# A two-layer RWKV-7 / mLSTM trunk on one core: group norm of a block at once, sums taken a step later, another order of addresses

## The chip, the core and the metric

The program runs on one core of a Trainium2 chip. A core has a matrix engine (PE, its weight loads are PEld), three engines for elementwise work (DVE, ACT, POOL), a queue that starts most transfers (SP), and 16 DMA engines. Each engine takes its instructions in the order in which they were written for it and waits on semaphores for the others. The metric is the device time of one execution in microseconds (us). Three runs of the kernel before took 2931.28, 2917.58 and 2933.17 us; the median is 2931.28 us.

## The reference

All of it is float32. The sequence is 1024 long, the width is 1024, there is one batch and there are two layers. A layer is a mixer and a SwiGLU feed-forward (FFN), each behind a modulated norm; layer 0 mixes by RWKV-7, layer 1 by a chunkwise mLSTM.

```
c_act = silu(c)
for i in 0, 1:
    sh1, sc1, g1, sh2, sc2, g2 = split(c_act @ ada_w[i] + ada_b[i], 6)   # modulation, a row of 6 x 1024
    x = x + g1 * mixer_i(rms(x) * (1 + sc1) + sh1)
    h = rms(x) * (1 + sc2) + sh2
    x = x + g2 * ((silu(h @ Wg) * (h @ Wu)) @ Wd)                       # inner width 2816
return rms(x) * final_w

# the end of the RWKV-7 mixer: a group norm over each head of 64
mu = mean(y, -1);  var = mean((y - mu)^2, -1)
y = (y - mu) * rsqrt(var + 64e-5) * gn_w + gn_b
out = ((y + bonus) * gate) @ w_out
```

## The kernel before, in words

Activations lie feature by position in tiles of 128 x 512: eight feature tiles `kt` and two halves of the sequence (`hf`, lists `x[0]` and `x[1]`). A float32 product is made of three passes over rounded parts: `split` (L209) writes a rounded copy on ACT (L211) and the remainder on DVE (L212), and `product` (L894) multiplies high by high, low by high and high by low. Weights come through the tile `wraw`, and their two parts lie in `wq` (or `whi`, `wlo`).

The stages follow each other in this order, by time in the profiled run:

- 0 to 305 us: modulation of layer 0, norms, projections of RWKV.
- 305 to 1019 us: the loop `chunks` (L1450). It has 19 steps. In step i the stages `rw_prep`, `rw_inverse`, `rw_solve`, `rw_chain` and `rw_finish` (L800) work on blocks i, i-1, i-2, i-3 and i-3, each 128 x 512; 16 blocks in all. Between the stages a generator of filler products (`fillers`, L1421) is run up to a quota: projections, and at the end the first FFN blocks that are computed ahead by `first` (L962) for half 0 alone, how many by the table `EARLY`.
- 1019 to 1680 us: output projection and FFN of layer 0 (`ffn`, L1064). Gate and up products are made by a scheme with seven sub-products (`seven`, L904) over tiles X[1] to X[7], which are sums and differences of quarter tiles, with weights from `wpair` (L865). Then comes `down` (L1003), again with seven sub-products.
- 1680 to 2141 us: mLSTM. 2141 to 2917 us: projection, FFN of layer 1 and the last norm (`final`, L1413).

Work that is not urgent runs as a background generator `self.bg`, a step at a time between weight loads: `sums` (L982) prepares weights for `down`, and `ada(s)` (L293) computes one sixth of the modulation of layer 1. `ada` loads 128 x 256 pieces of `ada_w`, adds them up on DVE with `c` as the factor (L305, L307; eight pieces to a sum), and sums over partitions with a small matmul against ones into the tile `tr`. It uses the tile `bgs` in the FFN stages and `st` in the others (`spare`, L289). `rstd` (L322) makes a norm: squares on ACT (L329) added on DVE (L330), four matmuls into `sc`, a power on POOL (L336), four more matmuls into `sc`.

`rw_finish` takes the 128 x 512 block `Ys`, eight groups of 64 columns. The mean comes from a reduction on DVE (L806). Then ACT makes the squares group by group with a summed output (L809, eight instructions and eight reads of the accumulator), POOL the power (L811), and ACT scales and shifts group by group (L814, eight instructions).

What sets the order: the program is written through a layer that gives each instruction a priority by its place in the program (parts under `ahead` are moved forward by the table `AHEAD`) and then lists each engine's instructions; a tile that is needed again waits for the last reader of whatever had its address. The tables `ROOM` and `FROOM` name the tiles of a phase with copies and columns; addresses are dealt out in the order of the table, so that a table's order says which tile of the next phase lies over which tile of the last. `phase` changes between them.

Of the kernel before, what the change touches and what calls it, by code (L numbers as in the profile page):

```python
# [9 lines left out]
F32 = mybir.dt.float32  # L10
# [7 lines left out]
P = 128  # L18
D = 1024
T = 1024  # L20
KT = 8
# [3 lines left out]
EARLY = ((0, 5, 8), (0, 0, 3))  # L25
# [20 lines left out]

RES = {"x": (8, 520)}
ROOM = {"wraw": (2, 1024), "whi": (2, 1024), "wlo": (2, 1024), "a": (18, 512), "KB": (1, 1024), "AT": (1, 512), "Z": (1, 512),
# [5 lines left out]
        "msq": (4, 2)}  # L54

FROOM = {"wraw": (3, 1024), "wq": (5, 2048), "w4": (2, 1024), "gb": (11, 1024), "bgs": (1, 1024), "tt": (5, 512),
# [73 lines left out]
class K:  # L130
# [158 lines left out]
    def spare(self):  # L289

        return self.t("bgs" if "bgs" in self.pools else "st", [P, 4, 256])

    def ada(self, s):  # L293

        nc = self.nc
        w, n = 256, 2
        for f in range(0, D, w):
            room = self.spare()
            t = room[:, 0]
            for kt in range(KT):  # L300
                m = room[:, 1 + kt % 3]
                nc.sync.dma_start(m, self.A["ada1"][kt, :, s * D + f:s * D + f + w])
                ca = self.ca[:, kt:kt + 1]
                if kt == 0:
                    nc.vector.tensor_scalar(t, m, ca, None, MUL)  # L305
                else:
                    nc.vector.scalar_tensor_tensor(t, m, ca, t, MUL, ADD)  # L307
                if kt % 2 and kt < KT - 1:
                    yield
            pt = self.bank("tr", [P, n])  # L310
            for q in range(n):
                self.mm(pt[:, q:q + 1], t[:, q * P:q * P + P], self.k_("ones"))
            u = 8 * s + f // P
            o = CI["adab1"] + u
            nc.vector.scalar_tensor_tensor(self.mod[1][:, u:u + n], pt, float(D), self.cc[:, o:o + n], MUL, ADD)
            if s in (1, 4):
                o = (0 if s == 1 else 8) + f // P
                nc.vector.tensor_scalar(self.scp[1][:, o:o + n], self.mod[1][:, u:u + n], 1.0, None, ADD)
            yield


    def rstd(self, xs):  # L322
# [477 lines left out]
    def rw_finish(self, S):  # L800
# [4 lines left out]
        m, v, jk = (self.t(n, [P, 64 if n == "gj" else 8]) for n in ("gm", "gv", "gj"))  # L805
# [879 lines left out]
```

## Time and profile before

| | |
|---|---|
| median of three runs | 2931.28 us (2917.58 to 2933.17) |
| the profiled execution | 2919.56 us |
| its span in the trace | 2917.8 us |
| PE / PEld busy | 2702.9 us (93%) / 2124.4 us |
| DVE / ACT / POOL busy | 2036.1 / 1401.1 / 74.5 us |
| moved by DMA | 492.38 MB, mean 169 GB/s |

The span is the time from the first instruction to the last; the profiled execution is 1.8 us longer than its span. Busy is the time in which an engine has an instruction at work, so 2917.8 less 2702.9, that is 214.9 us, is PE's idle time. [...] A row of the timeline that ends in brackets names how long the engine had been idle before it and what it waited for.

### The profile page before, as it was taken

How to read it: one execution, taken by the hardware profiler on the slowest of the kernel's cores; microseconds unless marked ns; L12 is line 12 of the kernel's file. 1: busy time of each engine (PE TensorE's matmuls, PEld its weight loads, DVE VectorE, ACT ScalarE, POOL GpSimd, SP SyncE). 2: the span in 40 equal slices, each digit the busy share in tenths (PEclk: the TensorE clock that was granted, in tenths of full speed). 3: DMA queues.
4: the chain of work that ended last, by engine and by line, in shares of the span. 5: the costliest groups of instructions: out<-in, count | busy, mean ns of one | idle time of the engine just before them, and what ended most of it. 6: DMA issues, size and time to landing. Idle time of an engine off the chain costs nothing.

```text
span 2917.8 us, 46574 instructions
## 1 busy us (share of the span) xinstructions
PE 2702.9 (93%) x17080; PEld 2124.4 (73%) x17080; DVE 2036.1 (70%) x4029; ACT 1401.1 (48%) x2641; POOL 74.5 (3%) x98
## 2 busy tenths in 40 slices
PE   6899889999898999999999989999989999999988
PEld 5576556677676677887777767778867788887776
DVE  7877776877676468788877677665556865667645
ACT  5766786777666554322244354233435433323433
POOL 0000000000000000000000000000000000000000
PEclk9899789999798999999999989889989999999999
DMA  8775444455543455577788744345264322347734
GB/s 293 262 266 149 121 128 125 119 158 145 155 138 102 134 199 163 187 228 233 243 276 258 229 138 129 121 152 159 94 205 146 106 100 94 107 138 246 237 118 150
DMA packets 359721, 492.38 MB, mean 169 GB/s; under 512 B 125212, under 2 KB 208796, under 8 KB 359492
## 3 DMA queue, kind: packets, MB, share of 16 engines
q1 hardware_dynamic: 345668, 464.24, 50.1%
q10 hardware_dynamic: 13824, 25.17, 2.4%
q8 instruction: 134, 2.20, 0.3%
q14 instruction: 95, 0.78, 0.1%
HBM read 359.77 MB, written 129.50 MB: 168 GB/s over the span
## 4 chain that ended last, share of the span: by engine, by line
PE 61%; DVE 14%; DMA 11%; ACT 6%; issue 6%; POOL 1%; SPq 1%; DVEq 0%; POOLq 0%; ACTq 0%
PE dn L207 23%; PE c L207 20%; PE iv L207 7%; PE px L207 7%; PE sc L207 2%; DMA wraw<-wsd 2%; DMA tt<-gd 1%; DMA wraw<-in_wdn 1%; DVE wq L212 1%; DMA bgs<-in_ada 1%; DVE ga L212 1%; ACT wq L211 1%; DVE wlo L212 1%; PE tr L207 1%; ACT whi L211 1%
## 5 line engine op out<-in xcount | busy, mean ns | idle before, releaser
L207 PE MATMUL dn<-a,whi 128*128 128x512 f32 (+1 forms) x1200 | 434.4, 428 | 20.4 <-ACT a L211 8.0
L211 ACT ACTIVATE wq<-wraw 128x1024 fp32r<-128x1024 f32 x202 | 210.7, 1057 | 335.4 <-DVE wraw L889 89.6
L207 PE MATMUL c<-ga,wq 128*128 128x512 f32 x1446 | 354.2, 394 | 8.6 <-ACT ga L211 7.8
L207 PEld LDWEIGHTS c<-ga,wq 128*128 128x128 f32 x1446 | 271.5, 189 | 73.7 <-ACT ga L211 10.1
L212 DVE TENSOR_TENSOR wq<-wraw,wq 128x1024 fp32r<-128x1024 f32 x202 | 244.3, 1221 | 85.3 <-ACT wq L211 85.1
L207 PEld LDWEIGHTS dn<-a,whi 128*128 128x128 f32 (+1 forms) x1200 | 226.3, 196 | 81.8 <-ACT a L211 10.7
L207 PE MATMUL dn<-a,wlo 128*128 128x512 f32 (+1 forms) x664 | 275.1, 425 | 5.8 <-ACT wlo L443 2.9
L207 PE MATMUL c<-gb,wq 128*128 128x512 f32 x894 | 220.9, 399 | 9.4 <-DVE wq L212 6.4
L207 PEld LDWEIGHTS c<-gb,wq 128*128 128x128 f32 x894 | 169.2, 191 | 49.5 <-DVE wq L212 7.6
L207 PEld LDWEIGHTS dn<-a,wlo 128*128 128x128 f32 (+1 forms) x664 | 128.8, 197 | 37.1 <-issue 4.8
L211 ACT ACTIVATE whi<-wraw 128x1024 fp32r<-128x1024 f32 (+2 forms) x96 | 100.4, 1046 | 113.2 <-PE dn L207 81.9
L212 DVE TENSOR_TENSOR wlo<-wraw,whi 128x1024 fp32r<-128x1024 f32 (+2 forms) x96 | 116.0, 1208 | 45.7 <-ACT whi L211 39.7
L207 PE MATMUL iv<-ga,wq 128*128 128x512 f32 x552 | 136.0, 389 | 0.0
L207 PE MATMUL px<-ga,wq 128*128 128x512 f32 x528 | 128.7, 389 | 0.0
L211 ACT ACTIVATE w<-wraw 128x384 fp32r<-128x384 f32 (+1 forms) x100 | 56.7, 567 | 139.9 <-PE c L207 62.3
L207 PEld LDWEIGHTS iv<-ga,wq 128*128 128x128 f32 x552 | 103.6, 188 | 21.6
L207 PEld LDWEIGHTS px<-ga,wq 128*128 128x128 f32 x528 | 99.1, 188 | 20.7
L207 PE MATMUL dn<-gb,wq 128*128 128x512 f32 x426 | 104.1, 396 | 5.0 <-ACT gb L211 4.7
L207 PE MATMUL iv<-gb,wq 128*128 128x512 f32 x432 | 104.7, 390 | 0.0
L207 PEld LDWEIGHTS dn<-gb,wq 128*128 128x128 f32 x426 | 81.1, 191 | 23.9 <-ACT gb L211 5.3
L207 PE MATMUL c<-ga,w 128*128 128x512 f32 x372 | 93.4, 393 | 1.1 <-DVE ga L212 0.7
L1124 ACT ACTIVATE x<-x 128x512 f32<-128x512 f32 x77 | 48.3, 629 | 95.0 <-DVE x L933 44.9
(607 smaller groups left out, 5643.5 us busy)
## 6 DMA issues: line engine op xcount, KB each, us to landing
wraw<-in_wgu SPq DMA_DIRECT2D x110, 512.0 KB, 3.5
tt<-gd SPq DMA_DIRECT2D x154, 256.0 KB, 4.1
KT<-in_ada SPq DMA_DIRECT2D x40, 512.0 KB, 5.3
gd<-x SPq DMA_DIRECT2D x77, 256.0 KB, 2.0
gd<-tt SPq DMA_DIRECT2D x72, 256.0 KB, 2.1
wraw<-wsd SPq DMA_DIRECT2D x32, 512.0 KB, 4.7
bgs<-in_ada SPq DMA_DIRECT2D x96, 128.0 KB, 3.3
wraw<-in_wdn SPq DMA_DIRECT2D x24, 512.0 KB, 4.4
```

The costliest lines, as they stand in the source:

```text
L207: return self.nc.tensor.matmul(out, lhsT, rhs, start=start, stop=stop, **kw)
L211: self.nc.scalar.activation(hi, src, AF.Copy)
L212: self.nc.vector.tensor_tensor(lo, src, hi.bitcast(F32), SUB)
L1124: nc.scalar.activation(t, t, AF.Silu)
```

## The change

Five things are changed. (1) `rw_finish` subtracts the mean from the whole block with one DVE instruction, squares it with one ACT instruction into a `pt` tile, reduces with one DVE instruction, and scales with one DVE instruction. (2) `ada` works in pieces of 128 x 128, two to a transfer, and takes each sum over partitions one step later, beside the next column's pieces. (3) `rstd` becomes a generator `rstd_steps`, whose three parts are put between products: in `ffn` between the products of the projection and of `first`, which became a generator too; in `down`, for `final`, between the last sub-products. The weights of the first `seven` are made (`wpair`) before X[4]. (4) The tables `ROOM` and `FROOM` are in another order, and in the mLSTM stage `x[1]` lies in `SA` and `pt` and no longer in `SR`. (5) `EARLY` computes six blocks ahead in the chunk loop (five before) and three in the FFN. The argument `halves` of `ml_so` changes nothing that is issued, since its test is never true.

```diff
-EARLY = ((0, 5, 8), (0, 0, 3))
+EARLY = ((0, 6, 9), (0, 0, 3))
-ROOM = {"wraw": (2, 1024), "whi": (2, 1024), "wlo": (2, 1024), "a": (18, 512), "KB": (1, 1024), ...
+ROOM = {"a": (18, 512), "mt": (3, 512), "AR": (4, 1024), "KT": (4, 1024), "wraw": (2, 1024), "whi": (2, 1024),
+        "wlo": (2, 1024), "st": (1, 1024), "ld": (3, 512), "KB": (1, 1024), ...
-FROOM = {"wraw": (3, 1024), "wq": (5, 2048), "w4": (2, 1024), "gb": (11, 1024), "bgs": (1, 1024), "tt": (5, 512),
+FROOM = {"gb": (11, 1024), "wraw": (3, 1024), "tt": (5, 512), "wq": (5, 2048), "w4": (2, 1024), "bgs": (1, 1024),
          "ga": (17, 1024), "rs": (1, 4)}
     def ada(self, s):
-        w, n = 256, 2
-        for f in range(0, D, w):
-            room = self.spare()
...
+        room = self.spare([P, 8, P])
+        def total(f):
+            pt = self.bank("tr", [P, 1])
+            self.mm(pt, room[:, f % 2], self.k_("ones"))
...
+        for f in range(KT):
+            t = room[:, f % 2]
+            for kt in range(0, KT, 2):
+                o = 2 + 2 * (kt // 2 % 3)
+                nc.sync.dma_start(room[:, o:o + 2], self.A["ada1"][kt:kt + 2, :, s * D + f * P:s * D + f * P + P]
+                                  .rearrange("k p w -> p k w"))
+                for k in range(2):
+                    m, ca = room[:, o + k], self.ca[:, kt + k:kt + k + 1]
+                    if kt + k == 0:
+                        nc.vector.tensor_scalar(t, m, ca, None, MUL)
+                    else:
+                        nc.vector.scalar_tensor_tensor(t, m, ca, t, MUL, ADD)
+                if kt % 4 == 2:
                     yield
...
+            if f:
+                total(f - 1)
+        yield
+        total(KT - 1)
-    def rstd(self, xs):
+    def rstd_steps(self, xs):
...
             nc.vector.tensor_tensor(acc, acc, sq, ADD)
+        yield
         pc = self.bank("sc", [P, 4])
...
         nc.gpsimd.tensor_tensor(r, r, self.mhalf[:, 0:4], POW)
+        yield
...
+        yield ps
+    def rstd(self, xs):
+        *_, ps = self.rstd_steps(xs)
         return ps
@@ rw_finish
         nc.vector.tensor_reduce(m, y3, mybir.AxisListType.X, ADD)
         nc.vector.tensor_scalar(m, m, -1.0 / 64, None, MUL)
-        for q in range(8):
-            nc.scalar.activation(jk, y3[:, q, :], AF.Square, bias=m[:, q:q + 1], accum_out=v[:, q:q + 1])
+        nc.vector.tensor_tensor(y3, y3, m[:, :, None].to_broadcast([P, 8, 64]), ADD)
+        sq = self.t("pt", [P, 8, 64])
+        nc.scalar.activation(sq, y3, AF.Square)
+        nc.vector.tensor_reduce(v, sq, mybir.AxisListType.X, ADD)
         nc.vector.tensor_scalar(v, v, 1.0 / 64, GN_EPS, MUL, ADD)
         nc.gpsimd.tensor_tensor(v, v, self.mhalf, POW)
-        nc.vector.tensor_tensor(m, m, v, MUL)
-        for q in range(8):
-            nc.scalar.activation(y3[:, q, :], y3[:, q, :], AF.Identity, bias=m[:, q:q + 1], scale=v[:, q:q + 1])
+        nc.vector.tensor_tensor(y3, y3, v[:, :, None].to_broadcast([P, 8, 64]), MUL)
@@ down
                     self.add_to(l, x, n, ps[n], to[p])
+                    next(rest, None)
...
             if p == 4:
-                done(0)
-        done(1)
+                rest = done(0)
+                next(rest, None)
+        for _ in done(1):
+            pass
@@ ffn
         if l == 1:
             self.store(0, x[0])
-            r = self.rstd(x[0])
-        second()
-        if l == 1:
-            self.norm_blocks(x[0], l, r)
+            r = self.rstd_steps(x[0])
+            for _ in range(2):
+                next(r)
+                next(two)
+            self.norm_blocks(x[0], l, next(r))
...
-        with self.ahead("norm"):
-            r = self.rstd(x[1])
+        r = self.rstd_steps(x[1])
...
+        head = some()
+        for _ in range(2):
+            next(r)
+            next(head)
+        run(head)
+        r = next(r)
...
+        order = [*range(n1, NH), *range(n1)]
+        w = wgu[l]
+        head = self.wpair(w[order[0]], w[order[0] + NH], order[0] >= n1)
         X[4] = []
...
-            sil = self.seven(self.wpair(w[n], w[n + NH], not there), X, "x", p[0])
+            sil = self.seven(head or self.wpair(w[n], w[n + NH], not there), X, "x", p[0])
+            head = None
@@ rooms
+        if ml:
+            return [t for _ in range(3) for t in self.two("SA", F32)] + [self.t("pt") for _ in range(2)]
```

What the change does to the order shows at three places. The first is PE in the FFN of layer 0, where the products of `first` end and `seven` begins; before, `dn_12314` is the last product of `first`, and `c_2025`, `iv_12437` and `c_2032` are of `seven`:

```order
L207 MATMUL dn_12314<-gb_11993,wq_12310 128x512 x3
L207 MATMUL dn_12314<-gb_11996,wq_12310 128x512 x3
L207 MATMUL dn_12314<-gb_11999,wq_12310 128x512 x3
L207 MATMUL c_2025_12422<-gb_11978,wq_12406 128x512 x2
L207 MATMUL iv_12437<-gb_11990,wq_12406 128x512 x2
L207 MATMUL c_2032_12494<-ga_12348,w_2022_12409 128x512 x2
```

Now, where `c_2016`, `c_2017` and the `dn` that follow are still of `first`, and `iv_12293` with the weights `wq_12220` is of `seven`:

```order
L208 MATMUL c_2016_12146<-gb_11553,wq_12143 128x512 x3
L208 MATMUL c_2016_12146<-gb_11556,wq_12143 128x512 x3
L208 MATMUL iv_12293<-gb_11559,wq_12220 128x512 x2
L208 MATMUL c_2017_12147<-gb_11559,wq_12143 128x512 x3
L208 MATMUL c_2017_12147<-gb_11562,wq_12143 128x512 x3
L208 MATMUL c_2017_12147<-gb_11565,wq_12143 128x512 x3
```

The first two matmuls of `seven` have moved ahead of the last 36 matmuls of `first`.

The second is the SP queue at the end of the mLSTM stage, where the results `yd` of both halves are stored (`yd_81`, `yd_82`) and the projection's inputs are loaded from `yd_81` into `tt`; before:

```order
L1372 DMA yd_81<-tmp_21025 128x512
L218 DMA wraw_21312<-in_wmo 128x1024
L218 DMA wraw_21343<-in_wmo 128x1024
L218 DMA wraw_21374<-in_wmo 128x1024
L218 DMA wraw_21405<-in_wmo 128x1024
L218 DMA wraw_21436<-in_wmo 128x1024
L218 DMA wraw_21467<-in_wmo 128x1024
L1372 DMA yd_82<-tmp_21119 128x512
L1372 DMA yd_82<-tmp_21127 128x512
L833 DMA tt_21210<-yd_81 128x512
```

Now:

```order
L1406 DMA yd_81<-tmp_21066 128x512
L847 DMA tt_21251<-yd_81 128x512
L847 DMA tt_21256<-yd_81 128x512
L847 DMA tt_21261<-yd_81 128x512
L847 DMA tt_21266<-yd_81 128x512
L847 DMA tt_21271<-yd_81 128x512
L219 DMA wraw_21353<-in_wmo 128x1024
L219 DMA wraw_21384<-in_wmo 128x1024
L219 DMA wraw_21415<-in_wmo 128x1024
L1406 DMA yd_82<-tmp_21160 128x512
```

Five loads of `tt` moved ahead of the last two stores of `yd_82`.

The third is ACT between the chunk loop and the projection, whose first matmuls read `ga_11692` (now `ga_11585`), while `gb` is for `first`; before:

```order
L211 ACTIVATE wq_11732<-wraw_11730 128x1024
L211 ACTIVATE gb_11978<-x_9249 128x512
L211 ACTIVATE gb_11981<-x_9251 128x512
L211 ACTIVATE gb_11984<-x_9253 128x512
L211 ACTIVATE gb_11987<-x_9255 128x512
L211 ACTIVATE ga_11692<-tt_11690 128x512
```

Now, from the seventh of eight `gb` on (`wq_11625` and six `gb` stand ahead of them):

```order
L212 ACTIVATE gb_11565<-x_9131 128x512
L212 ACTIVATE gb_11568<-x_9133 128x512
L212 ACTIVATE wq_11656<-wraw_11654 128x1024
L212 ACTIVATE wq_11687<-wraw_11685 128x1024
L212 ACTIVATE wq_11718<-wraw_11716 128x1024
L212 ACTIVATE ga_11585<-tt_11583 128x512
```

Four `gb` and three `wq` have moved ahead of the first `ga`.

## Rows read from the trace of the kernel before

**Rows 1.** The page, parts 1 and 4: engines, chain that ended last
```profile
PE 2702.9 (93%) x17080; PEld 2124.4 (73%) x17080; DVE 2036.1 (70%) x4029; ACT 1401.1 (48%) x2641; POOL 74.5 (3%) x98
...
PE 61%; DVE 14%; DMA 11%; ACT 6%; issue 6%; POOL 1%; SPq 1%; DVEq 0%; POOLq 0%; ACTq 0%
```

**Rows 2.** Stretches: us, busy PE, PEld, DVE, ACT, POOL, PEclk, DMA, GB/s
```profile
305.00:1019.00 714.00, 650.76 (x7350) 473.82 (x7349) 508.74 (x1307) 490.68 (x1197) 33.40 (x29) 0.91 0.45 131
1140.00:1413.00 273.00, 272.08 (x1189) 221.47 (x1188) 225.28 (x364) 76.02 (x100) 0.00 (x0) 1.00 0.67 217
1413.00:1660.00 247.00, 234.42 (x1002) 188.49 (x1001) 181.50 (x311) 96.02 (x140) 0.00 (x0) 0.97 0.80 261
1740.00:1865.00 125.00, 113.07 (x594) 91.35 (x595) 96.41 (x222) 45.14 (x79) 4.20 (x8) 0.91 0.41 127
1735.80:1749.50 13.70, 7.04 (x18) 5.25 (x19) 11.12 (x25) 6.02 (x9) 0.00 (x0) 0.50 0.42 119
2285.30:2288.70 3.40, 3.40 (x10) 2.65 (x9) 2.90 (x5) 0.56 (x2) 0.00 (x0) 0.51 0.00 0
```

**Rows 3.** Waits of PE, 305 to 1020: us, times, longest
```profile
PE c L207 <- ACT Ys L797: 7.5, 7, 4.5
PE iv L207 <- ACT Y L726: 6.4, 8, 1.1
PE c L207 <- DVE VU L787: 5.1, 7, 1.3
...
PE tr L817 <- ACT Ys L814: 4.0, 5, 1.5
```

**Rows 4.** Groups of 305 to 1020 (last two: whole span): busy, mean ns
```profile
L814 ACT ACTIVATE Ys<-Ys,gm,gv 128x64 f32<-128x64 f32 x128 | 45.5, 428 | 18.4 <-DVE gm L812 18.2
L809 ACT ACTIVATE gj<-Ys,gm 128x64 f32<-128x64 f32 x128 | 43.9, 343 | 11.2 <-DVE gm L807 9.0
L809 ACT ACTIVATION_READ_ACCUMULATOR gj<-Ys,gm 128x1 f32 x128 | 24.1, 188 | 0.0
L330 DVE TENSOR_TENSOR mt<-mt,mt 128x512 f32<-128x512 f32 x35 | 24.1, 688 | 2.1 <-ACT mt L329 0.9
L329 ACT ACTIVATE tt<-ga 128x512 f32<-128x512 f32 x21 | 13.0, 620 | 19.2 <-DVE ga L1058 16.6 <-DVE ga L841 2.5
```

**Rows 5.** Timeline of PE: start, us, instruction [idle before <-releaser]
```profile
1025.82 0.79 PE L207 MATMUL c<-ga,wq 128*128 128x512 f32 x1 [7.05 <-ACT ga L211]
1114.17 4.14 PE L207 MATMUL c<-gb,wq 128*128 128x512 f32 x10 [3.39 <-DVE wq L212]
1134.78 2.73 PE L207 MATMUL c<-gb,wq 128*128 128x512 f32 x6 [2.11 <-DVE x L933]
2284.28 3.34 PE L207 MATMUL c<-gb,wq 128*128 128x512 f32 x9 [3.04 <-DVE wq L212]
```

**Rows 6.** Line L307 (first row), line L1305 (second): xcount, duration ns min/median/max
```profile
L307 DVE SCALAR_TENSOR_TENSOR bgs<-bgs,ca x84: 472/480/487, 1418.7 to 1660.4; 128x256 f32<-128x256 f32 x84
L1305 DVE SCALAR_TENSOR_TENSOR pt<-sc,gj,br x32: 340/342/351, 1808.4 to 2111.6; 128x128 f32<-128x128 f32 x32
```

**Rows 7.** Waits of PE over the whole span, the sums of the modulation
```profile
PE tr L207 <- DVE bgs L307: 6.3, 4, 2.8
...
PE tr L207 <- DVE st L307: 3.1, 4, 1.4
```

**Rows 8.** Timeline of PE at the start and the end of the mLSTM stage
```profile
1740.22 1.22 PE L207 MATMUL dn<-AR,VU 128*128 128x512 f32 x2 [6.81 <-ACT VU L211]
2145.56 4.67 PE L207 MATMUL dn<-gb,wq 128*128 128x512 f32 x12 [4.73 <-ACT gb L211]
```

**Rows 9.** Timeline of three engines around the last norm of the first half
```profile
2833.30 2.32 SPq L1032 DMA_DIRECT2D tt<-gd  x5
...
2835.10 1.84 PE L207 MATMUL sc<-kc,bgs 128*128 128x1 f32 x8 [8.47 <-DVE bgs L330]
2836.30 0.63 ACT L211 ACTIVATE gb<-tt 128x512 fp32r<-128x512 f32 x1 [2.07 <-DMA tt<-gd]
```

More of the change, by code (lines that the diff above doesn't have):

```diff
@@ L287, in ada_rows, with spare @@
                 yield
-    def spare(self):
-        return self.t("bgs" if "bgs" in self.pools else "st", [P, 4, 256])
+    def spare(self, shape):
+        return self.t("bgs" if "bgs" in self.pools else "st", shape)
     def ada(self, s):
         nc = self.nc
-        w, n = 256, 2
-        for f in range(0, D, w):
-            room = self.spare()
[L299 to L308, printed above, removed]
-                    yield
[L310 to L319, printed above, removed]
@@ L976, in first @@
             out.append(t)
+            yield
         g, u = out
@@ L1026, in down @@
         ps = [None] * 4
+        rest = iter(())
         for i, p in enumerate((1, 6, 7, 2, 4, 5, 3)):
@@ L1068, in ffn @@
         _, n0, n1 = EARLY[l]
+        two = second()
         if l == 1:
             self.store(0, x[0])
-            r = self.rstd(x[0])
-        second()
-        if l == 1:
-            self.norm_blocks(x[0], l, r)
+            r = self.rstd_steps(x[0])
[3 more added lines that the diff above has]
+            self.norm_blocks(x[0], l, next(r))
         b11, b21 = self.parts(x[0][:4], "gb"), self.parts(x[0][4:], "gb")
+        for _ in two:
+            pass
         self.store(1, x[1])
-        with self.ahead("norm"):
-            r = self.rstd(x[1])
+        r = self.rstd_steps(x[1])
         tags = "tt", "tt"
@@ L1083, in some, with run @@
             if n0 < n1:
-                self.first(l, n0, b11 + b21, tags)
                 n0 += 1
-        some()
+                yield from self.first(l, n0 - 1, b11 + b21, tags)
+        def run(it):
+            for _ in it:
+                pass
+        head = some()
[4 more added lines that the diff above has]
+        r = next(r)
         X = {1: b11, 2: b21}
@@ L1096, in ffn @@
             X[6] += self.parts(f[3][kt:kt + 1], "ga")
-        some()
+        run(some())
         X[5] = self.parts(f[1], "ga")
@@ L1102, in ffn @@
             X[7] += self.parts(f[0][kt:kt + 1], "ga")
-        some()
+        run(some())
+        order = [*range(n1, NH), *range(n1)]
+        w = wgu[l]
+        head = self.wpair(w[order[0]], w[order[0] + NH], order[0] >= n1)
         X[4] = []
@@ L1108, in ffn @@
         while n0 < n1:
-            some()
+            run(some())
         self.rate = rates[0]
         self.background(2)
-        for n in chain(range(n1, NH), range(n1)):
+        for n in order:
             there = n < n1
-            w = wgu[l]
             p = [None] * 2
@@ L1271, in ml_v, with ml_so @@
         return va
-    def ml_so(self, n, hs):
+    def ml_so(self, n, hs, halves=(0, 1), out=None):
         wt = self.weights(self.A["wo"][n])
-        out = self.two("SR", F32)
-        for hf in range(2):
+        out = out or self.two("SR", F32)
+        for hf in halves:
             ps = self.bank("dn")
@@ L1414, in final @@
         nc = self.nc
-        r = self.rstd(xs[4:] + xs[:4] if hf else xs)
+        for r in self.rstd_steps(xs[4:] + xs[:4] if hf else xs):
+            if r is None:
+                yield
         for kt in range(KT):
@@ L1446, in fillers @@
         for n in range(EARLY[0][0], EARLY[0][1]):
-            self.first(0, n, hp, ("mt", "tmp"))
-            yield 11
+            for _ in self.first(0, n, hp, ("mt", "tmp")):
+                yield 5.5
     def chunks(self, x0):
@@ L1501, in load, with rooms @@
         return x
-    def rooms(self, hf):
+    def rooms(self, hf, ml=False):
         if hf == 0:
             return [self.t("x") for _ in range(KT)]
-        return [t for _ in range(4) for t in self.two("ga" if "ga" in self.pools else "SR", F32)]
+        if "ga" in self.pools:
+            return [t for _ in range(4) for t in self.two("ga", F32)]
+        if ml:
+            return [t for _ in range(3) for t in self.two("SA", F32)] + [self.t("pt") for _ in range(2)]
+        return [t for _ in range(4) for t in self.two("SR", F32)]
     def build(self):
@@ L1585, in second @@
             x[1] = self.load(self.rooms(1), 1, None if l == 0 else self.xd[1])
-            run(self.project(y, w, l, x[1], lambda: self.two("ga"), ("tt",)))
+            yield from self.project(y, w, l, x[1], lambda: self.two("ga"), ("tt",))
         self.bg = chain(self.sums(0), *(self.ada(s) for s in (1, 0, 2)))
-        self.ffn(0, x, lambda: second(self.yd[1], "wro", 0), lambda j: self.store(j, x[j]), (1, 1))
+        self.ffn(0, x, lambda: second(self.yd[1], "wro", 0), lambda j: iter([self.store(j, x[j])]), (1, 1))
         self.phase(ROOM)
@@ L1597, in build @@
         next(ml)
-        x[1] = self.load(self.rooms(1), 1, self.xd[1])
+        x[1] = self.load(self.rooms(1, True), 1, self.xd[1])
         nh[1] = self.normed(x[1], 1, 0, self.a1)
```

13 lines of the change are left out of this document (9 added, 4 removed), and 10 rows, old and new, of the table ROOM.

## The prediction

> **What bounds the kernel now.** I read the busy times first [rows 1]: PE is at work for 2702.9 of 2917.8 us, far more than DVE (2036.1) or ACT (1401.1), and the chain that ended last runs over PE for 61% of the span. No edit here takes a matmul away, so what can be won is PE's idle time, 214.9 us, and the time in which PE has half its clock. The stretches [rows 2] say where. From 1140 to 1413 us PE is busy for 272.1 of 273 at a clock of 1.00: nothing is to be had there. From 305 to 1019 us, the chunk loop, it is busy for 650.8 of 714, so 63 us are idle, and the clock is 0.91, which is (1 - 0.91) x 714 = 64 us of clock lost. One us of idle goes with about one us of clock there, so a wait removed can pay twice. Behind single long gaps the clock is at 0.50 for a while: 13.7 us behind the gap at the mLSTM's start, 3.4 us behind one at the head of the second FFN. Third, I read who ends PE's waits: in the chunk loop mostly ACT, with `Ys` and `Y` ahead [rows 3], and at the seams between stages single waits of 2 to 8 us [rows 5, 8, 9].
>
> **The change part by part.** The sum is made against the profiled execution, 2919.56 us, which lies 11.7 below the median of the runs.
>
> *Group norm, 16 blocks.* Removed from ACT in each block: eight squares, eight accumulator reads and eight scalings, in all blocks 43.9 + 24.1 + 45.5 = 113.5 us [rows 4]; added: one square of 128 x 512 in each, at 0.62 (L329) 9.9 us. ACT loses 103 us of its 491, a fifth. DVE gets three instructions over 512 columns, at 0.688 each by L330, and loses one small one of 0.16: 16 x 1.9 = +30 us on 509. The trace has no such instruction with a broadcast operand; L330 is the nearest row. So ACT, which PE waits for, is relieved, and DVE, at 71% of the stretch, goes to 75%. The three largest waits of PE for ACT come to 17.9 us. I let half of them go, as they are partly ACT's queue and partly true dependence (`Ys` comes out of a chain over DVE and ACT), and add 1 us on the DVE side, whose largest wait is 5.1: -8 us of idle, and at one for one nearly as much of clock: -15. The bounds are all 17.9 twice, -36, and the 30 us of DVE all on the path, +30. I choose -15 because the waits for ACT are the larger, and because a block's own chain gets shorter: 6.5 us less on ACT against 1.9 more on DVE.
>
> [...]
>
> *Modulation of layer 1 (`ada`).* The same bytes in as many transfers, with rows of 512 bytes instead of 1024. On DVE 192 instructions of 480 ns become 384 of about 342 (a like instruction over 128 columns, L1305) [rows 6]: 92 to 131, so +39 us, half in 1413 to 1660, half in the mLSTM stage. In 1413 to 1660 DVE goes from 181 to 201 of 247; in 1740 to 1865 from 96 to about 109 of 125 [rows 2]. In exchange the sum over partitions is asked for one step later, when DVE has long finished it: its waits of 6.3 and 3.1 us go [rows 7]. What is late next is the split of weights on DVE, for which the FFN has five tiles `wq`. I take -9 (the waits, nothing for clock). The bounds are -15, with the clock behind them, and +20, if the half of the 39 us that falls into the mLSTM stage holds up PE.
>
> *Heads of the FFNs.* In both layers the weights for the first `seven` are made while the last of `first`, or the additions for X[4], is still under way; the order shows matmuls of `seven` between those of `first`. The three waits, 3.39, 2.11 and 3.04 us [rows 5], were for exactly these weights and for `x` that DVE took up late behind them. With each go 3.4 us at half clock, worth 1.7. In all 13.6; I take -12, bounds -14 and 0.
>
> *Chunk loop to projection.* ACT now makes eight `gb` and three more `wq` before the first `ga`, which the first matmul waits for. `gb` lies over the tiles `a`, so its first waits for the last product of the loop. A `gb` takes ACT 0.63 us [rows 9]; a `wq` has twice the columns, by which I estimate 1.1. Eight `gb`, three `wq` and the first `ga` make 9 us, and with the release before and the matmul's start 9 to 10 of wait where 7.05 was [rows 5]; afterwards the `wq` are ready. +3, bounds -5 (the transfers that set the 7.05 are earlier now) and +8. One more FFN block by `first` in the loop, one less in the FFN: the same matmuls elsewhere, 0.
>
> *mLSTM.* At its start PE waits 6.81 us and then has half clock for 13.7, of which it works 7.0, so 3.5 more [rows 8, 2]. `x[1]`'s norm no longer takes turns with loads into `SR`, and its products stand together; but the norm's own chain through ACT and DVE stays, and each of the eight tiles still goes through it. I take half, -6, bounds -12 and 0. At its end PE waits 4.73 us for `gb`, whose inputs were loaded only after the last stores; five loads are now ahead of those. -5, bounds -5 and +2.
>
> *Norms between products.* In the second FFN the order still puts the norm's matmuls directly behind the last product, so nothing goes. The last norm of half 0 makes PE wait 8.47 us up to 2835.10, but the next products need `gb` from `tt`, whose loads were issued at 2833.30 and gave the first split at 2836.30 [rows 9]: the wait is hidden behind that anyway. The tail of PE and SP stands as before. 0.
>
> The sum: -15 - 9 - 12 + 3 - 6 - 5 = -44, which gives 2875.6 us on the profiled execution. A fresh run of the kernel before lies up to 14 us above it; I add 4, so that it stands between the profile and the median: **2880 us**.
>
> **The rivals.**
>
> *The loop gives nothing.* PE is busy for 91% of it, and what ACT leaves free the fillers already fill; the waits for `Ys` L797 come from DVE's `st` and remain. For it: the largest single wait, 4.5 us, is of that kind. Against it: the waits for L814 are of the removed instructions. Without the -15: 2895.
>
> *The loop gives much more.* All waits for ACT go, with their clock (-36 instead of -15), and the clock behind the modulation's waits too (-6). 2853. For it: 64 us of lost clock. Against it: DVE-ended waits stay, and each brings the clock down alike.
>
> *Only the seams change.* The loop and the modulation gain what DVE's load takes back, so -15 and -9 fall out, and the seam after the loop grows by 8 instead of 3 us. 2880 + 24 + 5 = 2909; with nothing at the mLSTM's start 2915. That includes the case that the change does not do what it says, as it already holds for the norms.
>
> *DVE becomes the bound: slower.* In the loop `rw_chain` and `rw_finish` run on DVE in one queue, and `VU` (waited for 5.1 us by PE) stands behind the new 512-column instructions, at 0.69 us each. From about the point where DVE is busy over 90% in the steps that matter, its 30 us count in full, and in the mLSTM, where 109 of 125 is near it, 20 of the 39. Then +30 + 20 - 12 + 3 - 6 - 5 = +30 on 2919.56 + 4: 2954. For it: of the group norm's five large steps four are now on DVE, where there was one. Against it: 75% in the loop.
>
> **How the numbers follow.** The forecast has 0.40, its own range 2862 to 2890; the loop gives nothing 0.22; much more 0.12; only the seams 0.16; slower 0.10. What a measurement of this kernel can tell from no change is about 0.5%, 14.7 us, so "same" is 2916.6 to 2946. The first three are faster, and of the seams' case about two in three lie above 2905 but only one in three above 2916. Faster: 0.40 + 0.22 + 0.12 + some 0.02 to 0.03 = 0.76, same 0.15, slower 0.09. The range for 8 in 10 goes from 2843, below which only part of the third case lies, to 2922, above which the slower case lies and a little of the seams'.
>
> **What would show it.** Right: in the profile after, ACT busy in the loop falls by about 100 us and DVE's rises by about 30; PE's idle time there falls from 63 to about 55 and its clock rises above 0.92; the waits of `tr` for `bgs` and `st` are gone; the waits for `wq` at the head of `seven` are gone; the gap behind the loop is 9 to 10 us; the gap before the first `gb` of the projection after the mLSTM is under 1 us; the gap at the last norm of half 0 is still about 8 us. Wrong: DVE-ended waits of PE in the loop that grow by more than 5 us, weight splits on DVE that PE waits for between 1740 and 1865 us, or a loop whose idle time is as before.

## The result: 0.6% slower, and the profile after

The changed kernel takes 2942.10 us (median of 12 runs), the kernel before 2927.76 on the same occasions; the ratio is 1.0059, with a 95% interval of 1.0044 to 1.0073. The ratio compares fast runs alone, so that a run of 3771.72 us of the kernel before does not enter it, and it is not quite that of the two medians. The forecast was 2880 with a range up to 2922, which the result lies above; it falls into the band that the prediction called "same" (2916.6 to 2946), but the interval is clear of no change. The profiled execution of the changed kernel has a span of 2938.8 us, 21.0 more than the one of before; the medians lie 14.3 apart, since the profiled execution of before is one of the faster. By the first instruction of each stage the difference lies here:

| stretch, by its first and last mark | before | after | difference |
|---|---|---|---|
| start to the first product of the layer 0 projection (start, RWKV loop) | 1025.8 | 1043.1 | +17.3 |
| to the first load of `down`'s weights (projection, gate and up) | 396.2 | 376.4 | -19.8 |
| to the first product of the mLSTM stage (`down`, `ada` beside it) | 276.4 | 293.3 | +16.9 |
| to the first product of the layer 1 projection (mLSTM, `ada` beside it) | 447.1 | 452.6 | +5.5 |
| to the end | 772.2 | 773.3 | +1.1 |

The first two belong together, because a block of 48 matmuls went from the second to the first; they make -2.5. What was lost in this pair of traces, 22.4 us, was lost where the modulation of layer 1 is computed; of the 16.9, 9.5 are two gaps at the seam in front of the mLSTM stage, shown below.

The first part of the page, after:

```profile
PE 2709.3 (92%) x17080; PEld 2129.5 (72%) x17080; DVE 2102.2 (72%) x4289; ACT 1329.6 (45%) x2276; POOL 73.8 (3%) x98
```

ACT has 72 us less to do and DVE 66 more; PE's idle time grew from 214.9 [rows 1] to 229.5 us. The stretches that answer to [rows 2], in the same columns:

```profile
305.00:1019.00 714.00, 649.55 (x7328) 471.44 (x7328) 530.39 (x1337) 409.08 (x825) 32.02 (x29) 0.90 0.46 132
1413.00:1660.00 247.00, 228.44 (x977) 181.53 (x976) 186.51 (x379) 93.79 (x137) 0.00 (x0) 0.98 0.79 252
1740.00:1865.00 125.00, 106.43 (x549) 83.70 (x548) 97.03 (x245) 58.25 (x82) 2.61 (x8) 0.92 0.35 106
```

In the loop ACT fell by 82 us and DVE rose by 22, yet PE is as busy as before (649.6 against 650.8) at nearly the same granted clock (PEclk, the share of full speed that PE was given: 0.90 against 0.91), so its idle time is as before. From 1413 to 1660 PE lost 6 us. There and from 1740 to 1865 DVE rose by 5.0 and 0.6 us only, where 20 and 13 had been reckoned: its work slid back beyond these windows. The waits of PE in the loop, after (us, times, longest), show where the loop's gain went; of before I add the three that were not shown:

```profile
PE tr L668 <- DVE KB L663: 9.1, 7, 2.6
PE sc L208 <- DVE SR L645: 5.8, 5, 1.5
PE c L208 <- ACT Ys L811: 5.7, 10, 1.1
PE sc L208 <- DVE AR L627: 4.7, 2, 2.7
...
PE iv L208 <- ACT Y L740: 3.4, 4, 0.9
PE c L208 <- DVE VU L801: 3.1, 5, 1.2
```

```profile
PE tr L654 <- DVE KB L649: 2.9, 2, 1.6
...
PE sc L207 <- DVE AR L613: 1.8, 1, 1.8
...
PE sc L207 <- DVE SR L631: 1.4, 2, 1.2
```

The waits for ACT's `Ys` and `Y` fell from 13.9 [rows 3] to 9.1 us and the 4.0 for L814 went. The waits for DVE's `KB`, `SR` and `AR` rose from 6.1 to 19.6: these are made in `rw_prep`, whose instructions stand in DVE's queue beside the group norm's. Not all waits for DVE rose: those for `VU` L787 (L801 now) fell from 5.1 to 3.1. Summed over all rows of the waits from 305 to 1000 us, PE waits 31.1 us for ACT and 27.0 for DVE before, 23.1 and 36.4 after. The norm's own instructions cost what was estimated:

```profile
L828 DVE TENSOR_TENSOR Ys<-Ys,gv 128x512 f32<-128x512 f32 x16 | 11.0, 690 | 19.0 <-POOL gv L827 19.0
...
L825 DVE TENSOR_REDUCE gv<-pt 128x8 f32<-128x512 f32 x16 | 10.9, 678 | 2.4 <-ACT pt L824 2.4
...
L822 DVE TENSOR_TENSOR Ys<-Ys,gm 128x512 f32<-128x512 f32 x15 | 10.3, 685 | 0.1
...
L824 ACT ACTIVATE pt<-Ys 128x512 f32<-128x512 f32 x16 | 10.0, 624 | 16.6 <-DVE KB L624 8.5 <-DVE Ys L822 7.7 <-DVE X L692 0.4
```

The modulation, which answers to [rows 6] and [rows 7]; the first row is of before:

```profile
L307 DVE SCALAR_TENSOR_TENSOR st<-st,ca x84: 446/478/486, 1671.0 to 1865.5; 128x256 f32<-128x256 f32 x84
...
L320 DVE SCALAR_TENSOR_TENSOR bgs<-bgs,ca x168: 339/350/356, 1440.8 to 1696.0; 128x128 f32<-128x128 f32 x168
L320 DVE SCALAR_TENSOR_TENSOR st<-st,ca x168: 317/350/355, 1703.4 to 1916.6; 128x128 f32<-128x128 f32 x168
```

```profile
PE tr L208 <- DVE bgs L320: 13.5, 13, 1.9
PE tr L208 <- DVE st L320: 12.1, 9, 3.6
```

Half the columns take 73% of the time, 350 ns against 480, as reckoned. But the waits of the sums, which were to go, rose from 9.4 to 25.6 us, and the last piece of `st` is added up at 1916.6, where it was at 1865.5 before. The places at the stages' seams, which answer to [rows 5] and [rows 8] (timeline of PE):

```profile
1043.13 1.22 PE L208 MATMUL c<-ga,wq 128*128 128x512 f32 x2 [7.98 <-ACT ga L212]
...
1130.88 4.63 PE L208 MATMUL c<-gb,wq 128*128 128x512 f32 x10 [3.63 <-DVE wq L213]
...
1707.82 2.08 PE L208 MATMUL sc<-kc,rs 128*128 128x128 f32 x8 [6.75 <-POOL rs L345]
1712.81 0.79 PE L208 MATMUL c<-a,VU 128*128 128x512 f32 x1 [2.70 <-ACT a L212]
...
1754.31 0.69 PE L208 MATMUL c<-a,wlo 128*64 128x512 f32 x1 [7.76 <-DVE wlo L213]
...
2165.45 1.20 PE L208 MATMUL dn<-gb,wq 128*128 128x512 f32 x2
...
2305.56 0.73 PE L208 MATMUL c<-gb,wq 128*128 128x512 f32 x2 [2.98 <-DVE tt L989]
```

At the heads of both FFNs one gap stands about as long as the old 3.39 and 3.04 (3.63 and 2.98); that of 2.11 is gone. In front of the mLSTM stage there is a gap that was not there, 6.75 us for the norm, and the old one of 6.81 is now 7.76 at another product. The gap in front of the layer 1 projection is gone.

All three signs that the prediction named for being wrong came: waits for DVE in the loop that grew by more than 5 us, a weight split (`wlo`) that PE waits for between 1740 and 1865 us, and a loop as idle as before.

### The profile page after: what moved, and what is told of

The parts are those of the page before. It is cut to its first block, busy times and chain, and to the rows that moved or that the text cites. A ratio compares the mean times of both kernels' runs of the same rounds, so it can differ in the third digit from the quotient of the medians.

```text
span 2938.8 us, 46407 instructions
## 1 busy us (share of the span) xinstructions
PE 2709.3 (92%) x17080; PEld 2129.5 (72%) x17080; DVE 2102.2 (72%) x4289; ACT 1329.6 (45%) x2276; POOL 73.8 (3%) x98
## 5 line engine op out<-in xcount | busy, mean ns | idle before, releaser
L208 PE MATMUL dn<-a,whi 128*128 128x512 f32 (+1 forms) x1216 | 444.2, 433 | 17.9 <-ACT a L212 9.4
L208 PE MATMUL c<-ga,wq 128*128 128x512 f32 x1566 | 381.4, 394 | 13.9 <-ACT ga L212 12.2
L208 PEld LDWEIGHTS c<-ga,wq 128*128 128x128 f32 x1566 | 295.4, 190 | 80.6 <-ACT ga L212 14.7
L208 PE MATMUL dn<-a,wlo 128*128 128x512 f32 (+2 forms) x672 | 281.5, 429 | 3.4 <-ACT tmp L434 2.0
L208 PE MATMUL c<-gb,wq 128*128 128x512 f32 x858 | 211.2, 398 | 8.6 <-DVE wq L213 5.5
L208 PEld LDWEIGHTS dn<-a,wlo 128*128 128x128 f32 (+2 forms) x672 | 132.7, 200 | 35.5 <-issue 4.2
L208 PE MATMUL dn<-ga,wq 128*128 128x512 f32 x462 | 114.0, 395 | 0.0
L208 PE MATMUL iv<-gb,wq 128*128 128x512 f32 x456 | 112.3, 394 | 0.0
L208 PEld LDWEIGHTS dn<-ga,wq 128*128 128x128 f32 x462 | 87.9, 191 | 18.8 <-DVE ga L213 0.4
L208 PEld LDWEIGHTS iv<-gb,wq 128*128 128x128 f32 x456 | 87.1, 191 | 18.8 <-DVE x L947 0.3
```

The lines of the kernel that those rows point to most:

```text
L208: return self.nc.tensor.matmul(out, lhsT, rhs, start=start, stop=stop, **kw)
```

## The experiments

Each ran 5 to 12 times; ratios are to the kernel before on the same chip. They ran on five chips, so that experiments are compared with each other by their ratios. Edits are shown in short, without the lines that only follow from them, and some comments in them are added here. A second reading of the changed kernel itself, on the chip of three of the experiments, gave a lower ratio than the first, so its cost is 0.4 to 0.6%.

**The changed kernel again.** No edit.

> The changed kernel itself, word for word, on the chip that runs the experiments beside it, so that they can be held against it: 1.0059 times the kernel before, by both theories, some 2950 us if the kernel before stands at 2932.

Measured: 2942.32 us, 1.0037 (1.0020 to 1.0054). The interval overlaps with the first one; experiments are held against both.

**Old modulation in the changed kernel.**

```diff
-        for f in range(KT):            # 128 columns, two pieces to a load, sum one step later
+        for f in range(0, D, 256):     # 256 columns, sum behind the last piece
```

> The changed kernel with the modulation of layer 1 (ada) as before: pieces of 128 x 256, four sums to a sixth, each taken right behind its last piece. Theory A (it is the number of sums: 48 instead of 24 places where PE has to wait for DVE, which is late because its pieces land late): PE's waits of tr for bgs and st fall from 25.6 to about 9 us, and the time by 12 to 20, to 2922 to 2930. Theory B (it is DVE's load, 39 us more for the same sums): the same sign, but the gain sits in other waits for DVE too, and tr's waits fall by less than half. Theory C (the modulation is hidden, as the prediction's sum had it): no change or slower by up to 9 us.

Measured: 2933.57 us, 1.0005 (0.9989 to 1.0021). All of the loss is gone. The waits of `tr`:

```profile
PE tr L208 <- DVE bgs L308: 9.1, 7, 2.4
...
PE tr L208 <- DVE st L308: 3.8, 4, 1.4
```

They fell by half, to 12.9. A and B are both allowed by this; C is not.

**New modulation alone, in the kernel before.** The edit of the section on the change, `ada` only.

> The kernel before with the new ada alone (pieces of 128 x 128, eight sums to a sixth, each a step later). Theory B (the doubled number of DVE instructions makes DVE late where PE waits for it): 8 to 16 us slower than the kernel before, PE's waits of tr above 20 us, ada's last piece in the mLSTM stage some 40 us later. Theory of the prediction: 9 us faster, tr's waits gone. If it is neutral alone, the cost needs the other parts (the addresses).

Measured: 2942.74 us, 1.0051 (1.0031 to 1.0071). The modulation by itself makes the kernel as slow as the whole change does. Its sums wait as in the changed kernel, 23.2 us:

```profile
PE tr L207 <- DVE bgs L319: 12.1, 13, 1.8
...
PE tr L207 <- DVE st L319: 11.1, 9, 3.6
```

**Half as many sums, same pieces.**

```diff
-            if f:
-                total(f - 1)
+            if f % 2:
+                total(f - 1)           # two columns, behind the second's last piece
```

> The changed kernel with ada in the same 128 x 128 pieces and the same transfers, but the sums over partitions of two columns taken together, right behind the second column's last piece: 24 places on PE instead of 48, DVE's load as in the changed kernel. Theory A (each sum is a place where PE waits for DVE, so their number counts): tr's waits fall from 25.6 to about 13 us, 8 to 12 us faster than the changed kernel. Theory B (DVE's 39 us more are what counts): within 4 us of the changed kernel, tr's waits stay above 20 us or come back in other waits for DVE.

Measured: 2963.96 us, 1.0111 (1.0089 to 1.0132): slower than the changed kernel, with waits of `tr` of 37.8 us at half the places. Fewer sums didn't help, so their number (theory A) is not the cause. Theory B missed too: at the same DVE instructions on the pieces it is 0.7% above the changed kernel on the same chip (1.0037). This kernel also lacks the lag of a step, so with pieces of 128 the lag may well help; the two were changed together and were not told apart.

**Old pieces, with the lag.** The edit is shown against the old `ada`; the two accumulators leave room for one piece less loaded ahead.

```diff
-            pt = self.bank("tr", [P, n])           # behind kt == 7
+                if kt == 3 and g:
+                    total(g - 1)                   # half a column of 256 later
```

> The changed kernel with ada in pieces of 128 x 256 as before the change, but each sum half a column's pieces later, as the change meant it. 24 places on PE, DVE's load as before the change. Theory A (number of places; the list puts each sum where it reckons DVE to be done, so the lag in the program buys little): like the changed kernel with the old ada, 12 to 17 us faster than the changed kernel, tr's waits 9 to 13 us. Theory C (the lag itself is worth its waits, the prediction's reading): tr's waits under 4 us, 20 to 26 us faster than the changed kernel. Theory B (DVE's load) gives the same time as A, but pieces of 128 with half the sums would then gain nothing.

Measured: 2932.43 us, 1.0006 (0.9988 to 1.0023), `tr` waits 11.6 us. As with the old modulation: at 256 columns the lag, with the shorter run of loads, is worth nothing, against the prediction's reading (theory C).

**Old loads and sums, DVE cut in two.** The edit is shown against the changed kernel with the old modulation.

```diff
+                for h in range(0, w, P):
+                    th, mh = t[:, h:h + P], m[:, h:h + P]
-                    nc.vector.scalar_tensor_tensor(t, m, ca, t, MUL, ADD)
+                        nc.vector.scalar_tensor_tensor(th, mh, ca, th, MUL, ADD)
```

> The changed kernel with the transfers and sums of the old ada (128 x 256 pieces, rows of 1024 bytes, four sums to a sixth), but each DVE instruction cut into two of 128 columns, as many as in the changed kernel. Theory B (DVE's load, 39 us more): within 4 us of the changed kernel, 8 to 16 us slower than with the old ada. Theory D (the short rows of 512 bytes make the pieces land late): like the old ada, 1.000 to 1.002 times the kernel before.

Measured: 2937.33 us, 1.0035 (1.0023 to 1.0047), against 1.0005 with whole instructions. Nothing but the number and width of DVE's instructions differs, so their cost is shown: 0.3%, some 9 us. DVE's busy time in the two stages with the modulation, from the first load of `down`'s weights to the layer 1 projection, grew by 21.8 us for it (479.6 to 501.4); in the new modulation alone the multiply-adds kept DVE busy for 36.5 us more (80.6 to 117.1), and that cost 0.5%, some 15 us: in both about 0.4 us of time for one of DVE, an estimate from single traces. The cost doesn't sit in the sums, whose waits are short here:

```profile
PE tr L208 <- DVE bgs L310: 6.5, 7, 1.5
...
PE tr L208 <- DVE st L310: 1.1, 3, 0.7
```

In the mLSTM stage PE's waits for DVE, summed over all rows, are 34.8 us against 27.8 with whole instructions; 6.8 of them are one wait for `wlo`. The difference of up to 0.2% to the whole new modulation, and of 0.8% to the kernel with half the sums, may lie in the rest of DVE's load (the first), in the short rows or in where the sums stand; that was not told apart.

**Wider pieces in the mLSTM stage, in the kernel before.**

```diff
-        w, n = 256, 2
+        w = 512 if wide else 256       # wide: where the tile is st
-    "st": (1, 1024)
+    "st": (1, 1536)
```

> The kernel before with ada the other way in the mLSTM stage: pieces of 128 x 512, half as many DVE instructions and half as many sums there as before the change (st has 1536 columns, so one piece less is loaded ahead). If DVE's instructions for the modulation are what PE waits for in that stage (theory B), about 10 us less DVE work is worth 3 to 8 us: the mLSTM stage shorter than 447 us, 0.997 to 0.999 times the kernel before. If the cost of the narrow pieces has another cause, or DVE is late only beyond some load, no change; if the shorter run of loads ahead counts, slower.

Measured: 2916.33 us, 0.9964 (0.9946 to 0.9981): faster than both kernels. The direction is theory B's, but the cause is not shown by this run: transfers and sums of that stage were halved too, rows made longer and addresses moved, and PE's waits for DVE in the stage did not fall (26.6 us before, 33.2 here, with one of 7.5 for `wlo` at the place where 6.8 for ACT's `VU` had been). The mLSTM stage of six kernels, from its first product to the first of the projection behind it (columns as in the stretches above): the kernel before, the new modulation alone, the old modulation in the changed kernel, the same with DVE cut in two, wider pieces, and the new group norm alone (below):

```profile
1698.40:2145.60 447.20, 405.41 (x2223) 327.97 (x2222) 287.51 (x717) 174.70 (x361) 27.39 (x39) 0.92 0.44 139
```

```profile
1705.20:2169.10 463.90, 409.80 (x2225) 329.02 (x2223) 304.55 (x822) 185.88 (x370) 26.44 (x39) 0.90 0.43 134
```

```profile
1711.00:2155.10 444.10, 410.15 (x2224) 332.46 (x2225) 285.17 (x712) 175.72 (x363) 26.97 (x42) 0.92 0.42 136
```

```profile
1711.00:2162.60 451.60, 413.80 (x2224) 334.19 (x2225) 297.42 (x802) 179.37 (x365) 25.21 (x42) 0.90 0.43 134
```

```profile
1699.80:2140.00 440.20, 399.55 (x2218) 324.22 (x2218) 278.08 (x661) 174.27 (x361) 26.82 (x39) 0.93 0.44 139
```

```profile
1705.60:2159.00 453.40, 409.68 (x2222) 331.21 (x2221) 287.72 (x716) 174.51 (x362) 27.39 (x39) 0.91 0.44 137
```

DVE's busy time is the third figure behind the length. Held against the kernel that they were made from, the stage grows with it: by 16.7 us for 17 (new modulation), 7.5 for 12 (DVE cut in two), and it shrinks by 7.0 for 9 (wider pieces); PE's clock falls and rises with it, between 0.93 and 0.90. But these are single traces, and the stage is not set by DVE's load alone: with the new norm, which does not touch this stage, it took 453.4 us at the 288 us of the kernel before, and with one entry of `ROOM` moved (below) 465.2 at 300, where the changed kernel has 452.7 at 302. No slope can be read from them.

**Old group norm in the changed kernel; new group norm alone.** The edit of `rw_finish`, taken out of the one and put into the other.

> The changed kernel with the group norm of before (ACT group by group). Theory A (the loop is bound by its chain over PE, DVE and ACT together; what ACT is relieved of comes back as waits for DVE): ACT busy in the loop rises by some 80 us, the time by no more than 4 either way, 2938 to 2946. Theory B (the prediction's: the new group norm does help by 15 us, and other parts hide it): slower by 10 to 18, 2952 to 2960. Theory C (the new group norm costs, DVE is the bound): faster by 5 to 12, 2930 to 2937.

> The kernel before with the new group norm alone. Theory A (ACT's relief comes back as waits for DVE, on which three more 512-column instructions stand in each block): ACT busy in the loop falls by 80 us or more, PE's idle time there stays within 5 us, and the time is between 4 us faster and 8 slower. Theory B (the prediction's): 12 to 18 us faster. Theory C (DVE's 30 us count in good part): 8 to 20 us slower.

Measured: 2938.83 us, 1.0021 (1.0004 to 1.0038), and 2930.36 us, 1.0014 (1.0000 to 1.0028). By the first the new norm costs 0.2 to 0.4% in the changed kernel, by the second 0.1% in the kernel before; both are hardly clear of noise, and that it gains 15 us is excluded. The loop, 305 to 1000 us, of the kernel before and with the new norm alone:

```profile
305.00:1000.00 695.00, 633.49 (x7275) 460.31 (x7275) 501.35 (x1294) 480.07 (x1166) 31.76 (x28) 0.90 0.45 131
```

```profile
305.00:1000.00 695.00, 631.05 (x7297) 458.52 (x7282) 520.98 (x1320) 404.28 (x818) 29.34 (x28) 0.90 0.45 129
```

76 us of ACT gone, 20 of DVE added, PE's busy time and clock the same: theory A, with at most a small loss. The sums of PE's waits moved as in the changed kernel, from 31.1 to 23.9 us for ACT and from 27.0 to 36.8 for DVE. The wait for `KB` grew here too:

```profile
PE tr L654 <- DVE KB L649: 9.5, 7, 2.7
```

Whether `KB` comes late through DVE's queue or through tiles was not told apart: the new square takes one of the four `pt` tiles, of which `rw_prep` uses five in turn, and ACT waited 8.5 us for `KB` before that square in the changed kernel.

**The old order of ROOM in the changed kernel.** The table's lines of before, `FROOM` as changed.

> The changed kernel with the order of addresses of before in the table ROOM alone. Theory A (the new order lays the first weight tile of the mLSTM stage over weight tiles that PE still reads, so its load starts only with the last product of the FFN): the gaps of 6.75 and 2.70 us at 1701 and 1710 us go, with 13.7 us of half clock behind them, worth some 9 + 6 us; at the end of the mLSTM stage the inputs of the projection come late again, 4 to 5 us back. Net 8 to 12 us faster, 2930 to 2934. Theory B (addresses do not matter, DVE's load does): within 3 us of 2942.

Measured: 2953.05 us, 1.0068 (1.0041 to 1.0094). No gain. PE's wait of 6.75 us for `rs` went (the longest for `rs` is 2.3 us here), but where the changed kernel waits once for the squares `mt`, 16.6 us at its start, this one waits three times, 24.3 us in all with a longest of 16.8. By this mixture of tables `mt` lies over tiles `wq` of the FFN; so the experiment didn't isolate what it meant to.

**One entry of ROOM moved.**

```diff
-ROOM = {"a": (18, 512), "mt": (3, 512), "AR": (4, 1024), ... "Y1": (1, 258), "rs": (2, 4), ...
+ROOM = {"a": (18, 512), "mt": (3, 512), "rs": (2, 4), "AR": (4, 1024), ...
```

> The changed kernel with one entry of ROOM moved: the four-column tile rs (eight columns in all) stands behind mt instead of near the end. Theory A (at its new address rs lies over the last ga tile of the FFN, which is written and stored last, so the norm that opens the mLSTM stage can't finish before the FFN has): PE's gap of 6.75 us before sc<-rs at 1701 us and the 2.70 behind it go, with about 14 us of half clock; 10 to 15 us faster than the changed kernel on this chip, that is about 2935 to 2940 if that stands at 2950. Theory B (the seam is late because DVE is behind with the modulation's pieces; the address of rs is innocent): the norm is asked for earlier, but its waits turn up before or after it: within 4 us of the changed kernel.

Measured: 2945.03 us, 1.0052 (1.0031 to 1.0073), as the changed kernel. The address was the reason for the gap: with `rs` elsewhere the norm's wait is gone, and two others stand at the seam (timeline of PE):

```profile
1711.25 0.38 PE L207 MATMUL tr<-kc,bgs 128*128 128x1 f32 x2 [3.57 <-DVE bgs L319]
...
1715.26 6.94 PE L207 MATMUL c<-a,VU 128*128 128x512 f32 x22 [2.92 <-DVE VU L212]
```

The stretch from the first load of `down`'s weights to the first product of the mLSTM stage is 6.7 us shorter than in the changed kernel (286.6 against 293.3), but the stage itself is 12.6 longer (465.2 against 452.6), and the time is the same. Why it became longer is not shown.

**Both remedies, and the old group norm on top.** The edits for the old modulation and `rs`; then these and the old `rw_finish`.

> The changed kernel with the old ada and with rs at an address that comes free early. Theory B (DVE's load in the mLSTM stage took back what the earlier norm gave; with the old ada DVE has room): the seam's 9 us and part of its half clock are now worth something: 6 to 14 us faster than with the old ada alone, 0.996 to 0.999 times the kernel before. If the seam is worth nothing in any case: as with the old ada alone, 1.0005.

> As the one before it, and with the old group norm too. What is left of the change is then the order of the norms and of the heads, the tables of addresses and the block computed ahead. Theory A (the group norm is about neutral): within 5 us of the one before it. Theory C (it costs 8 to 12): 0.992 to 0.996 times the kernel before, the fastest of all.

Measured: 2929.79 us, 1.0004 (0.9991 to 1.0018), and 2925.09 us, 0.9998 (0.9984 to 1.0012). The seam is worth nothing with the old modulation either (1.0005 without the edit of `rs`), so DVE's load of the modulation is not what took its gain back. All the rest of the change, the heads, the norms between products, the addresses (but `rs`) and the block moved, comes to nothing together.

**Blocks computed ahead.** Five in the changed kernel; six in the kernel before; seven in the last variant.

```diff
-EARLY = ((0, 6, 9), (0, 0, 3))
+EARLY = ((0, 5, 8), (0, 0, 3))       # the others: (0, 6, 9) for (0, 5, 8); (0, 7, 10) for (0, 6, 9)
```

> The changed kernel with five FFN blocks computed ahead in the loop instead of six (48 matmuls, some 11 us, go back into the FFN). Theory A (neutral): within 3 us of 2942. Theory B (the sixth block runs at the loop's end with nothing beside it, and its waits and the wait for the projection behind it cost): faster by 4 to 8, 2934 to 2938.

> The kernel before with the sixth FFN block computed ahead in the loop, alone. By the stages of the changed kernel with five and with six blocks (11.1 us more at the loop's end, 18.6 less in the first FFN): 5 to 9 us faster than the kernel before, 0.997 to 0.998. By the prediction: 0.

> The changed kernel with the old ada, the old group norm, rs at an early address, and seven blocks computed ahead in the loop and three in the FFN. If each block moved is worth 5 to 9 us: 0.996 to 0.998 times the kernel before. If the sixth block's gain was that of one gap alone: as with six, 0.9998, or slower, since more products stand at the loop's end.

Measured: 1.0068 (1.0045 to 1.0091), 0.9998 (0.9980 to 1.0017), 1.0011 (0.9995 to 1.0026). Moving a block is worth nothing that can be measured, as predicted. The 7 us that I had read from the stages of two single traces were not there.

**The last variant with wider pieces.** Old group norm, `rs` moved, `ada` as in the wider pieces above.

> The changed kernel with the old group norm, rs at an early address and ada as in the one before it (256 columns in the FFN stage, 512 in the mLSTM stage). Theory B: 3 to 8 us faster than with the old ada, 0.997 to 0.999 times the kernel before; otherwise 0.9998 as that one.

Measured: 2921.36 us, 0.9968 (0.9949 to 0.9987), against 0.9998 without. The gain repeats in another arrangement, though the two intervals overlap by a little, with an mLSTM stage of 440.5 us instead of 445.5.

## Why the prediction was wrong, step by step

**The modulation is the step that failed.** It is the one part that clearly made the kernel slower; the gains of three other parts, which did not come, make up the larger share of the 58 us between the forecast sum of -44 and the +14 measured. I took -9 us: the sums, asked for "one step later, when DVE has long finished it", would no longer wait, and DVE's 39 us would be covered by free time on DVE. The runs say +0.3 to +0.5%, 9 to 15 us, for this part alone. Its instructions and durations were counted about rightly (its multiply-adds kept DVE busy for 36.5 us more). Two readings were wrong. The price of DVE's added time was put at nothing from the busy share: DVE at 64 to 74% looked free, but cutting its instructions in two, with transfers and sums as they were, cost 0.3%, some 9 us; neither nothing nor the full length. And the lag in the program was taken for a lag on the engine: the sums wait 25.6 us where they had waited 9.4. That they stand behind DVE work that is itself late fits the last piece, 51 us later, but was not tested by itself, and the kernel with half the sums (1.0111) shows that something beyond DVE's load counts, which stays open. The bound that I gave, +20, held this; I chose the wrong end. Pieces of 128 lose 0.3 to 0.5% here, and pieces of 512 in the mLSTM stage went with 0.4% less (0.9964).

**The loop: -15 predicted, +2 to +4 measured, hardly clear of noise** (1.0004 against 0.9998 in the kernels with both remedies, and 1.0014 for the norm alone). ACT's relief was 76 us in 15 blocks, where 103 had been reckoned in 16 and so 97 in 15. The 113.5 us were the sum of the busy times of three groups, and two of these overlap: an accumulator read starts 0.24 us into a square of 0.34, so that by estimate 0.1 us at each of 120 reads, 12 us, was counted twice. Where the other 9 us are is not shown. The waits for ACT fell, by 7 us. What failed is the step from there to PE: the waits for DVE, most of all in `rw_prep`, rose by 10. The rival "the loop gives nothing" described it, and "DVE becomes the bound" named the engine, at 75%; the 90% from which I let it decide was a guess of mine that no run shows.

**Heads of the FFNs: -12 predicted, about 0.** The order moved as described, but a wait of 3.63 and one of 2.98 us stand there still, for other tiles from DVE. No run has this part alone; it is within the rest that came to nothing together (0.9998).

**mLSTM: -11 predicted, about 0.** The wait at its end went as predicted. At its start a wait came that I had overlooked, by the address of `rs`, whose columns by the tables lay over the last `ga` tile of the FFN. Moving `rs` took the wait away and did not change the time; the wait at the end was not tested by itself.

**Right were** the seam behind the loop (7.98 us and another 1.47, for 9 to 10) and the block moved (0). The norms between products were put at 0, which no run contradicts; the last norm's wait of half 0 is shorter than foretold, 4.71 us for about 8.

The chance of slower, 0.09, was too low: the sum added five gains, and each took a wait that goes for time won, though another wait, mostly for DVE, could take its place.

## What to carry to other kernels

A share of 64 to 74% did not make DVE free here: PE waited for it in many short stops (26.6 us in the mLSTM stage before, none longer than 3.6), and work added to it was paid in part, about 0.4 us for one of busy time, the estimate made above from two pairs of traces. Test such a share with one cheap experiment, cutting or joining the engine's instructions with all else equal, before gaps are counted as gains. A gap taken away on PE was not yet time won: twice here another wait, or a longer stage behind it, took its place (with the new norm alone the loop's waits for ACT fell by 7.2 us and those for DVE rose by 9.8; with `rs` moved one stretch was 6.7 us shorter and the next 12.6 longer). And one trace of a stage wasn't enough to find a few us: the mLSTM stage differed by 6 us (447.2 and 453.4) between kernels that do the same in it.

## What had not been expected of the hardware

A DVE instruction over 512 columns with an operand broadcast along groups of 64 took 685 to 690 ns, as one without broadcast (688): the broadcast cost nothing here. A multiply-add over 128, 256 and 512 columns took 350, 480 and 745 ns, so that one over 512 takes about half the time of four over 128. Neighbours on ACT and DVE overlap: an accumulator read started 0.24 us into a square of 0.34, eight scalings of 0.43 each took 2.76 us in a row, and the multiply-adds cut in two were 35 us longer as a sum of durations but kept DVE busy for 18 us more. So sums over such instructions overstated what an engine was relieved of or loaded with.
